# Both expert stages of a two-layer diffusion block in groups of four experts of one token stream

## The chip, the cores and the metric

The kernel runs on one core of one Trainium2 chip. The metric is the device time of one execution in microseconds; the profile's span, from the first to the last instruction, lies inside it.

## The reference, cut to the expert stage

A layer is a mixer (attention or a recurrence) followed by a mixture of experts. Layer 0 runs the experts on two token streams of 256 tokens each (context and latent), layer 1 on the latent stream alone. Each token goes to 2 of 32 experts; an expert is a gate, an up and a down matrix of 1024 x 256, 1024 x 256 and 256 x 1024 in fp32.

```python
def hier_moe(h, w_rg, b_rg, w_re, b_re, w_gate, w_up, w_down):
    ...
    y = jnp.zeros_like(x)
    for g in range(MOE_GROUPS):
        a = jax.nn.silu(jnp.einsum('td,edf->tef', x, w_gate[g])) * jnp.einsum('td,edf->tef', x, w_up[g])
        y = y + jnp.einsum('tef,efd->td', a * comb[:, g, :, None], w_down[g])
    return y.reshape(b_, n, d)

def reference(...):
    for layer in range(DEPTH):
        ...
        x = x + g1 * o_lat
        x = x + g2 * hier_moe(ada_modulate(x, norm2_g[layer], sh2, sc2), *moe_p)
        if not last:
            xc = xc + g1c * o_ctx
            xc = xc + g2c * hier_moe(ada_modulate(xc, norm2_g[layer], sh2c, sc2c), *moe_p)
    return rmsnorm(x, final_norm_g)
```

## The kernel before

The expert stage (`moe`) does not run every token through every expert. Each expert has 32 slots (`CAP`) per stream. `gather` multiplies one-hot matrices with the normed tokens and so collects the tokens of eight (layer 0) or four (layer 1) experts as columns of a tile `X`. `experts` works on a *pack*, 128 columns of `X`: in layer 0 two experts with 64 columns each, 32 of either stream; in layer 1 four experts with 32 columns.

- **Gate and up** (L1670, tile `gu`): `X` is the stationary operand, 128 x 64 in layer 0 and 128 x 32 in layer 1; the expert's weight streams past it, 256 columns. Matmuls of two experts alternate (`for j in es`, two entries), so two column blocks of the array work side by side. A matmul in fp32 is two instructions in the trace.
- **Turn** (`aT`, L1680): the product of gate and up is transposed.
- **Down** (L1697, tile `y`): stationary 128 x 32, 512 columns stream past. In layer 0 four blocks are side by side (two streams of two experts), in layer 1 two.
- **Scatter** (L1748, tile `sc`): `y` times the gate vector is split into a high and a low fp32r part, which in layer 0 stand on the upper and lower 64 partitions of one tile `z`, so that one matmul with a selection matrix brings both back to the tokens; VectorE adds the result to `x` (L1751). In layer 1, fp32 without a split.

Weights come by `fetch` (L1483), one DMA of 1 MiB each, issued by SyncE (SP) in the order of `start_loads`: `g g u u` of two experts at a time, the `d` of a pack after the `g` and `u` of the next one. They land in a rotation of *slots* of 1 MiB (`wm`): load number i takes the slot of load i minus the number of slots, and SP waits until the matmuls that read that slot are done. In layer 0 there are 14 slots (rings of 4 and 4, and `YRING` 6), in layer 1 21. All but one are filled ahead of a test (`tc.If(cnt > cap)`, L1453) on whether any expert has more than 32 tokens of a stream. In these inputs none has, and the body of the test, which repeats the work for the surplus, is skipped; every engine passes the test. What follows the end of the body needs every semaphore at the count that the body would have left.

The instructions are put in order on each engine by a scheduler with a simulated timeline of its own; it may move a load past the test.

Of the kernel before, what the change touches and what calls it, by code (L numbers as in the profile page):

```python
# [15 lines left out]
P = 128  # L16
# [76 lines left out]
class K:  # L93
# [3 lines left out]
    YRING = (6, 2)  # L97
    YG = 1
# [7 lines left out]
    OH = (1, 2)  # L106
    ET = (1, 1)
    ZP = 0
    XP = 1
    WP = (0, 2)  # L110
    YS = 1
# [11 lines left out]
    AB = 1  # L123
# [223 lines left out]
    def gate2(self, layer):  # L347
        self.g2 = self.cst.tile([P, D], F32, name="g2", tag="ms25")
        h = P // (2 - layer)
        for n, c in enumerate((0,) if layer else (1, 0)):  # L350
            self.nc.sync.dma_start(self.g2[n * h:n * h + h], cv2(self.md[layer], c * 4 * D + 3 * D, [[0, h], [1, D]]))
# [137 lines left out]
    def outproj(self, layer, wout, tiles):  # L489
# [81 lines left out]
        side = self.gather(self.rv, [0, 1], self.X, part=[0]) if layer == 0 else iter(())  # L571
# [669 lines left out]
    GRP = (256, 128)  # L1241
# [4 lines left out]
    def moe_open(self, layer):  # L1246
# [6 lines left out]
        self.cw = self.S * self.CAP  # L1253
        self.ne = P // self.cw
        self.grp = self.GRP[layer]
# [140 lines left out]
    def moe(self, layer):  # L1396
        nc = self.nc
        V = nc.vector
        cap, nt, ne = self.CAP, self.nt, self.ne
# [10 lines left out]
        cmx = self.counts()  # L1410

        n, m = 32 * self.cw // self.grp, self.grp // P

        def whole(rv):
            self.rank_rows(rv)
            w = 2 - layer
            groups = [list(range(t, t + w)) for t in range(0, n, w)]
            X = self.X
            old, prev = iter(()), iter(())
            for g, nxt in zip(groups, groups[1:] + [[]]):  # L1420
                gen = self.gather(rv, nxt, X) if nxt else iter(())
                packs = [(t, pk) for t in g for pk in range(m)]
                for t, pk in packs:
                    cur = self.experts((t * m + pk) * ne, X[t], pk, ne, self.load)
                    next(cur)
                    drain(old)
                    next(prev, None)
                    next(cur)
                    if layer:
                        for _ in range(KD // m):  # L1430
                            next(gen, None)
                    elif (t, pk) == packs[-1]:
                        drain(gen)
                    old, prev = prev, cur
                drain(gen)
            next(old, None)
            next(prev, None)
            drain(old, prev)

        def more(rv, grp):  # L1440
            self.rank_rows(rv)
            for t in range(grp * m, grp * m + m):
                X = {}
                self.over = self.px.tile([P, 2, 1024], F32, name="over", tag="yl")
                drain(self.gather(rv, [t], X, over=True))
                drain(self.experts(t * ne, X[t], 0, ne, self.load_one))

        if not layer:
            drain(self.gather(self.rv, [0, 1], self.X, part=[1]))
        elif self.GF:  # L1450
            drain(self.gather(self.rv, [0], self.X))
        cnt = nc.values_load(cmx[0:1, n:n + 1], min_val=0, max_val=2 * P)
        with self.tc.If(cnt > cap):  # L1453
            rv2 = p.tile([P, nt, 32], F32, name="rv2")
            V.tensor_copy(rv2, self.rv)
            for grp in range(n):
                es = slice(grp * 32 // n, (grp + 1) * 32 // n)
                cg = nc.values_load(cmx[0:1, grp:grp + 1], min_val=0, max_val=2 * P)
                with self.tc.For_i(cap, cg, cap):
                    V.tensor_scalar_add(rv2[:, :, es], rv2[:, :, es], -float(cap))  # L1460
                    more(rv2, grp)
        self.prefetch(1)
        if layer and not self.GF:
            drain(self.gather(self.rv, [0], self.X))
        whole(self.rv)
# [93 lines left out]
    def ranks(self, s):  # L1559
# [12 lines left out]
        g = 32 * self.cw // self.grp  # L1572
        V.tensor_reduce(self.cm[:, s, :g], pc[:, :32].rearrange("p (g e) -> p g e", g=g), axis=AX.X, op=ALU.max)

    def counts(self):
        V, p = self.nc.vector, self.mp
        g = 32 * self.cw // self.grp
# [17 lines left out]
    def gather(self, rv, ts, out, over=False, part=None):  # L1595
        nc, p = self.nc, self.p
        cap, nt, S, cw, ne = self.CAP, self.nt, self.S, self.cw, self.ne
        part = list(range(S) if part is None else part)
        grp = P if over else self.grp
        n1, m = grp // cw, grp // P  # L1600
        n, e0 = n1 * len(ts), n1 * ts[0]
        if ts[0] not in out:
            for t in ts:
                q, tag = (self.px, "xt0") if S == 1 else (self.mp, f"xt{t % 2}")
                out[t] = (self.over[:, 0].rearrange("p (k c) -> p k c", k=KD) if over else q.tile([P, KD, grp], F32, name="X", tag=tag, bufs=1),
                          self.mp.tile([P, m], F32, name="ws", tag="wso" if over else "ws", bufs=4), {})
        X, ws, oh = out[ts[0]]
        for s in part:
            both = self.mp.tile([P, 2, n, cap], F32R if S > 1 else F32, name="onehot", tag="oh0", bufs=nt // 2)
            for i in range(0, 2, self.OH[self.layer]):  # L1610
                j = slice(i, i + self.OH[self.layer])
                nj = self.OH[self.layer]
                nc.vector.tensor_tensor(both[:, j], self.iob[:, :cap].unsqueeze(1).unsqueeze(1).to_broadcast([P, nj, n, cap]),  # L1613
                                        rv[:, 2 * s + i:2 * s + i + nj, e0:e0 + n].unsqueeze(3).to_broadcast([P, nj, n, cap]), op=ALU.is_equal)
            oh[2 * s], oh[2 * s + 1] = both[:, 0], both[:, 1]
        for k in range(KD):
            o = self.ps("xg")[:, :len(part) * n * cap]
            for q, s in enumerate(part):
                os = o[:, q * n * cap:(q + 1) * n * cap]
                for i in (2 * s, 2 * s + 1):  # L1620
                    r = oh[i].rearrange("p e s -> p (e s)")
                    hs = [self.h2h[:, i, k]] + ([self.h2l[s][:, i % 2, k]] if S > 1 else [])
                    for n_, h in enumerate(hs):
                        nc.tensor.matmul(os, h, r, start=i % 2 == 0 and n_ == 0, stop=i % 2 == 1 and n_ == len(hs) - 1)  # L1624
            q0 = k - (KD - m * len(ts))
# [155 lines left out]
```

## Time and profile before

| | before |
|---|---|
| device time, three runs | 1153.53, 1154.44, 1156.45 us |
| span of the profiled execution | 1152.0 us |
| TensorE (PE) busy | 1033.0 us, 90% |
| VectorE (DVE), ScalarE (ACT), GpSimd busy | 603.2, 426.1, 250.2 us |
| read from HBM | 292.98 MB, 255 GB/s over the span |
| layer 0's expert matmuls | from 390.5 us to about 660 us |
| layer 1's expert matmuls | from 904.2 us to the end |

The profiled execution has no device time of its own beside its span; the median of the three runs is 2.4 us above the span. Times in the trace are microseconds from the start of the span. Matmul ends in the trace are modelled, so how fast a group of matmuls runs is read from starts: the start of the group to the start of what follows.

### The profile page before, as it was taken

The numbers are of one execution on the slowest core, as the hardware profiler recorded it, in microseconds if no ns is written. First come the engines' busy times: TensorE is split into PE (matmuls) and PEld (weight loads), VectorE is DVE, ScalarE is ACT, GpSimd is POOL, SyncE is SP. The second block draws the span as 40 slices with busy tenths as digits, with TensorE's granted clock in tenths as the row PEclk, the third lists the DMA queues.
The fourth block names the chain that finished last, engine by engine and source line by source line (L and its number), as shares of the span: only waits on it lengthen the run. The fifth ranks groups of instructions, "written<-read, shape, count | busy, mean of one in ns | idle before, by whom it ended". The sixth has DMA issues, their size and how long they took to land. (4 is left out here: it accounts for less than half of the span.)

```text
span 1152.0 us, 19666 instructions
## 1 busy us (share of the span) xinstructions
PE 1033.0 (90%) x7917; PEld 644.9 (56%) x7917; DVE 603.2 (52%) x1261; ACT 426.1 (37%) x769; POOL 250.2 (22%) x283
## 2 busy tenths in 40 slices
PE   4998796979896699999999787999997799999996
PEld 3766573757674456565564365566654565444442
DVE  4349776577467347686667851344676122212223
ACT  4354455547545323242232352446555110000002
POOL 2216463426306000000000165343420000000000
PEclk9999798989998799999999989999999899999999
DMA  9883435344445299999979756642477599999920
GB/s 307 278 303 134 161 125 198 110 154 145 148 176 232 98 418 376 423 406 371 420 319 343 226 172 181 216 168 110 136 232 318 219 420 419 420 422 419 420 83 37
DMA packets 99183, 295.57 MB, mean 257 GB/s; under 512 B 23000, under 2 KB 57040, under 8 KB 74368
## 3 DMA queue, kind: packets, MB, share of 16 engines
q1 hardware_dynamic: 97360, 292.64, 67.7%
q10 hardware_dynamic: 1200, 1.26, 0.4%
q8 instruction: 67, 1.10, 0.4%
q0 software_dynamic: 512, 0.21, 0.1%
q14 instruction: 44, 0.36, 0.1%
HBM read 292.98 MB, written 1.11 MB: 255 GB/s over the span
## 5 line engine op out<-in xcount | busy, mean ns | idle before, releaser
L1670 PE MATMUL gu<-g,X 128*64 128x256 f32 (+1 forms) x1024 | 126.9, 392 | 9.0 <-DVE rq L1588 4.7
L1697 PE MATMUL y<-d,aT 128*32 128x512 f32 x768 | 131.6, 596 | 0.2
L1751 DVE TENSOR_TENSOR x<-sc,x 128x512 f32<-128x512 f32 x156 | 99.5, 685 | 50.1 <-PE sc L1748 49.9
L1670 PE MATMUL gu<-u,X 128*64 128x256 f32 (+1 forms) x1024 | 120.6, 380 | 0.0
L1735 POOL COPY esel<-idb 32x64 bf16<-32x64 bf16 (+1 forms) x40 | 11.2, 300 | 439.3 <-PE bc L1736 397.5
L1670 PEld LDWEIGHTS gu<-g,X 128*64 128x64 f32 (+1 forms) x1024 | 67.3, 126 | 54.0 <-issue 12.4
L1670 PEld LDWEIGHTS gu<-u,X 128*64 128x64 f32 (+1 forms) x1024 | 68.4, 123 | 44.3 <-issue 3.2
L1675 ACT ACTIVATE sge<-gu 128x256 f32<-128x256 f32 x24 | 9.2, 384 | 190.6 <-PE gu L1670 190.6
L1624 PE MATMUL xg<-onehot,h2h 128*128 128x128 f32 (+1 forms) x384 | 68.5, 294 | 3.6 <-DVE onehot L1613 1.7
L1697 PEld LDWEIGHTS y<-d,aT 128*32 128x32 f32 x768 | 31.9, 109 | 70.4 <-issue 62.9
L1748 PE MATMUL sc<-z,sc 128*128 128x512 f32 x184 | 65.2, 482 | 4.0 <-DVE z L1727 4.0
L183 PE MATMUL pt<-hh,wl 128*128 128x512 f32 (+1 forms) x160 | 61.2, 383 | 7.6 <-POOL wl L177 6.4
L181 PE MATMUL pt<-hh,wh 128*128 128x512 f32 (+1 forms) x160 | 63.7, 398 | 1.2 <-ACT hh L430 0.6
L1634 ACT ACTIVATE X<-xg,ab 128x128 f32<-128x128 f32 x104 | 42.0, 458 | 61.4 <-PE xg L1624 43.6
L1624 PEld LDWEIGHTS xg<-onehot,h2h 128*128 128x128 f32 x384 | 57.0, 200 | 13.3 <-issue 8.8
L1676 DVE SCALAR_TENSOR_TENSOR sge<-gu,ws,sge 128x256 f32<-128x256 f32 x24 | 11.5, 479 | 96.5 <-ACT sge L1675 96.5
L182 PE MATMUL pt<-hl,wh 128*128 128x512 f32 (+1 forms) x160 | 60.7, 379 | 0.8 <-DVE hl L432 0.8
L1725 ACT CAST z<-yg 64x512 fp32r<-64x512 f32 x64 | 39.5, 617 | 48.9 <-DVE yg L1719 44.2
L1636 DVE TENSOR_SCALAR X<-xg,ab 128x128 f32<-128x128 f32 x88 | 33.0, 407 | 46.9 <-PE xg L1624 46.1
L177 POOL TENSOR_TENSOR wl<-wcol,wh 128x512 fp32r<-128x512 f32 (+1 forms) x32 | 41.1, 1288 | 55.7 <-ACT wh L174 54.9
L1727 DVE TENSOR_TENSOR z<-yg,z 64x512 fp32r<-64x512 f32 x64 | 43.9, 686 | 17.3 <-ACT z L1725 16.0
L1748 PEld LDWEIGHTS sc<-z,sc 128*128 128x128 f32 x184 | 31.9, 189 | 33.5 <-issue 17.7
(402 smaller groups left out, 2056.3 us busy)
## 6 DMA issues: line engine op xcount, KB each, us to landing
g<-in_moe_w_gate_dram SPq DMA_DIRECT2D x64, 1024.0 KB, 10.8
u<-in_moe_w_up_dram SPq DMA_DIRECT2D x64, 1024.0 KB, 11.9
d<-in_moe_w_down_dram SPq DMA_DIRECT2D x64, 1024.0 KB, 11.3
wada<-in_ada_w_dram SPq DMA_DIRECT2D x48, 1024.0 KB, 6.2
wcol<-in_ab_w_in_dram SPq DMA_DIRECT2D x8, 1024.0 KB, 8.8
wcol<-in_cd_w_in_dram SPq DMA_DIRECT2D x5, 1024.0 KB, 12.0
wtok<-in_ab_w_in_dram SPq DMA_DIRECT2D x4, 1024.0 KB, 5.5
wout<-in_ab_w_out_dram SPq DMA_DIRECT2D x4, 1024.0 KB, 8.7
```

The costliest lines, as they stand in the source:

```text
L177: (el or nc.vector).tensor_tensor(lo, src, hi.bitcast(F32), op=ALU.subtract)
L181: mm(out, lh, rh, start=start, stop=False, **kw)
L182: mm(out, lh, rl, start=False, stop=False, **kw)
L183: mm(out, ll, rh, start=False, stop=stop, **kw)
L1624: nc.tensor.matmul(os, h, r, start=i % 2 == 0 and n_ == 0, stop=i % 2 == 1 and n_ == len(hs) - 1)
L1634: nc.scalar.activation(xv[:, s], o[:, j, q], AF.Identity, scale=a2, bias=b2)
L1670: A.matmul(pg[r, c0:c0 + 256], X[:, k, (pk * ne + j) * cw:(pk * ne + j + 1) * cw], ws[j][:, k % (KD // parts), :], start=k == 0 and c0 == ...
L1697: A.matmul(py[hf][r:r + cap, :], aT[:, k, q:q + cap], ws[j][:, k - k0, hf * 512:(hf + 1) * 512], start=k == 0, stop=k == 1)
L1725: S.copy(Z[s][a, cs], yg[a])
L1727: eng.tensor_tensor(Z[s][b, cs], yg[a], Z[s][a, cs].bitcast(F32), op=ALU.subtract)
L1748: A.matmul(o, sc[:, n * P:(n + 1) * P], z[:, cs], start=z is zs[0] and not last, stop=z is zs[-1])
L1751: V.tensor_tensor(self.xi(i)[:, cs], o, self.xi(i)[:, cs], op=ALU.add)
```

## The change

Both layers work on *quads*, four experts of one stream: 128 columns are 4 experts x 32 slots of one stream. A quad in layer 0 has both streams one after the other, each with its own `X`, `gu`, `aT`, `y` and `z`. Gate, up and down all have 128 x 32 stationary operands and four blocks side by side. The high and low parts of `z` are two tiles of 128 partitions, whose two matmuls add up in the accumulator. The first quad's gate and up in layer 0 stand ahead of the test, stream by stream. `YRING` goes from 6 to 4 in layer 0, which leaves 12 slots. Loads come as `g` x4, `u` x4, then the `d` x4 of the quad before. The second stream's gate vector is a tile of its own (`g2b`), loaded from GpSimd's queue.

```diff
-    YRING = (6, 2)
+    YRING = (4, 2)
+    NQ4 = 8
+    ZB = 4
...
     def start_loads(self, layer, head):
-        ne = P // ((2 - layer) * self.CAP)
         self.order = []
-        for e0 in range(0, 32, ne):
-            for h in range(e0, e0 + ne, 2):
-                self.order += [(k, h + j) for k in "gu" for j in range(2)]
-            if e0:
-                self.order += [("d", e0 - ne + j) for j in range(ne)]
+        for q in range(self.NQ4):
+            self.order += [(k, 4 * q + j) for k in "gu" for j in range(4)]
+            if q:
+                self.order += [("d", 4 * q - 4 + j) for j in range(4)]
...
+        if layer:
+            drain(self.gather(self.rv, 0, 4, 0, self.X))
+            cur = None
+        else:
+            drain(self.gather(self.rv, 0, 8, 1, self.X))
+            cur = self.quad(0, self.X, segs, self.load)
+            self.gate_up(cur, by_seg=True)
+        cnt = nc.values_load(cmx[0:1, nq:nq + 1], min_val=0, max_val=2 * P)
         with self.tc.If(cnt > cap):
...
+        for q in range(nq):
+            end = q == nq - 1
+            if cur is None:
+                cur = self.quad(q, self.X, segs[::-1] if end else segs, self.load)
+                self.gate_up(cur)
+            Q[q], cur = cur, None
+            if S > 1 and q % 2 and not end:
+                for s in segs:
+                    drain(self.gather(self.rv, 4 * q + 4, 8, s, self.X))
+            if q > 1:
+                self.scatter(Q[q - 2], segs)
+            if q:
+                self.down(Q[q - 1], segs)
+            self.turned(Q[q])
+            if S == 1 and not end:
+                drain(self.gather(self.rv, 4 * q + 4, 4, 0, self.X))
+        self.scatter(Q[nq - 2], segs[::-1])
+        for s in segs[::-1]:
+            self.down(Q[nq - 1], [s])
+            self.scatter(Q[nq - 1], [s])
...
+        def mms(key, c0, s, k0, ws):
+            X, _, q0 = st["X"][s]
+            x0 = (q - q0) * P
+            for k in range(k0, k0 + kn):
+                for j, w in ws.items():
+                    A.matmul(pg[s][32 * j:32 * j + 32, c0:c0 + 256], X[:, k, x0 + 32 * j:x0 + 32 * j + 32], w[:, k - k0, :],
+                             start=k == 0 and c0 == 0, stop=k == KD - 1, skip_group_check=True)
...
+        if by_seg:
+            ws = {key: {j: load(key, 4 * q + j) for j in range(4)} for key in "gu"}
+            for s in segs:
+                for key, c0 in (("g", 0), ("u", 256)):
+                    mms(key, c0, s, 0, ws[key])
+                mid(s)
+            return
+        for h in range(0, 4, step):
+            for key, c0 in (("g", 0), ("u", 256)):
+                for k0 in range(0, KD, kn):
+                    ws = {j: load(key, 4 * q + j, k0, k0 + kn) for j in range(h, h + step)}
+                    for s in segs:
+                        mms(key, c0, s, k0, ws)
...
+                z = (zz[:, hf * D:hf * D + D] if last else p.tile([P, D], F32R, name="z", tag="z", bufs=self.ZB)).rearrange("p (a c) -> p a c", a=2)
+                yg = self.yg[:, cs] if last else p.tile([P, 512], F32, name="yg", tag="yg", bufs=2)
+                V.tensor_tensor(yg, py[s, hf], self.g2[s][:, cs], op=ALU.mult)
+                self.split(yg, z[:, 0], z[:, 1])
+                st["z"][s, hf] = [z[:, 0], z[:, 1]]
...
+                    for m, z in enumerate(zs):
+                        nc.tensor.matmul(o, st["sc"][:, n * P:(n + 1) * P], z, start=m == 0 and not last, stop=m == len(zs) - 1)
+                    if not last:
+                        nc.vector.tensor_tensor(self.xi(i)[:, cs], o, self.xi(i)[:, cs], op=ALU.add)
```

**SP at the test of layer 0.** The load queue of the kernel before: the last two loads issued ahead of the test, the test, the end of its body, and the first loads behind it (`g_5`, `u_4`: gate of expert 5, up of expert 4; the brackets name the queues and engines that a row waits for).

```order
L1483 DMA g_5_3555<-in_moe_w_gate_dram 128x2048 [waits DMAHW5_49]
L1483 DMA u_4_3557<-in_moe_w_up_dram 128x2048 [waits DMAHW6_49]
L1452 TENSOR_LOAD cmx [waits DVE_49]
L1453 COMPARE_AND_BRANCH
...
L1453 UNCONDITIONAL_BRANCH [waits SP_sequencer_49,DMAHW0_49,DMAHW1_49,DMAHW2_49,DMAHW3_49,DMAHW4_49,DMAHW5_49,DMAHW6_49,DMAHW7_49]
L1483 DMA u_5_7520<-in_moe_w_up_dram 128x2048 [waits DMAHW2_49,DMAHW6_49,DVE_49,DMAHW7_49,PE_49,Activation_49]
L1483 DMA d_2_7715<-in_moe_w_down_dram 128x2048 [waits DMAHW0_49,PE_49]
```

The same place of the changed kernel.

```order
L1479 DMA g_6_3562<-in_moe_w_gate_dram 128x2048 [waits DMAHW3_49]
L1429 TENSOR_LOAD cmx [waits DVE_49]
L1479 DMA u_4_7531<-in_moe_w_up_dram 128x2048 [waits DMAHW4_49,PE_49]
L1479 DMA u_5_7533<-in_moe_w_up_dram 128x2048 [waits DMAHW5_49,PE_49]
L1479 DMA u_6_7535<-in_moe_w_up_dram 128x2048 [waits PE_49]
L1479 DMA u_7_7537<-in_moe_w_up_dram 128x2048 [waits DMAHW7_49,PE_49]
L1479 DMA d_0_7757<-in_moe_w_down_dram 128x2048 [waits DMAHW0_49,PE_49]
L1479 DMA d_2_7761<-in_moe_w_down_dram 128x2048 [waits DMAHW2_49,PE_49]
L1430 COMPARE_AND_BRANCH
...
L1430 UNCONDITIONAL_BRANCH [waits SP_sequencer_49,DMAHW0_49,DMAHW1_49,DMAHW2_49,DMAHW3_49,DMAHW4_49,DMAHW5_49,DMAHW6_49,DMAHW7_49]
L1479 DMA g_7_7444<-in_moe_w_gate_dram 128x2048 [waits DMAHW2_49,DVE_49,DMAHW3_49,PE_49,Activation_49]
```

Seven loads (`u_4` to `u_7`, `d_0` to `d_2`) now stand between the reading of the count and the test, and `g_7`, which the second quad's gate needs first, stands behind the end of the body, where SP waits for all eight hardware queues.

**PE behind the test of layer 0**, changed kernel: the first quad's transposes, three of the second quad's four gates twice, then rows that do not need `g_7` (left out are 20 matmuls of the next gather), then `g_7`.

```order
L1683 MATMUL aT<-ident,sge 128x128
L1651 MATMUL gu<-g_4_3558,X 32x256 [waits DVE_49,DMAHW1_49,PE_49,Activation_49]
L1651 MATMUL gu<-g_5_3560,X 32x256 [waits DMAHW2_49]
L1651 MATMUL gu<-g_6_3562,X 32x256 [waits DMAHW3_49]
L1651 MATMUL gu<-g_4_3558,X 32x256 [waits PE_49]
L1651 MATMUL gu<-g_5_3560,X 32x256
L1651 MATMUL gu<-g_6_3562,X 32x256
L1584 LDWEIGHTS rq [waits DVE_49]
...
L1651 MATMUL gu<-g_7_7444,X 32x256 [waits DMAHW3_49]
L1651 MATMUL gu<-g_4_3558,X 32x256
```

In the kernel before, the first pack's gate (`g_0`, `g_1`) stands at this place; in the changed one the whole first quad's gate and up stand ahead of the test.

**PE in layer 1**, gate matmuls of experts 20 to 23 in the kernel before and of 16 to 19 in the changed one.

```order
L1670 MATMUL gu<-g_21_14611,X 32x256
L1670 MATMUL gu<-g_20_14609,X 32x256
L1670 MATMUL gu<-g_21_14611,X 32x256
L1670 MATMUL gu<-g_20_14609,X 32x256
L1670 MATMUL gu<-g_21_14611,X 32x256
```

```order
L1651 MATMUL gu<-g_18_14440,X 32x256
L1651 MATMUL gu<-g_19_14442,X 32x256
L1651 MATMUL gu<-g_16_14436,X 32x256
L1651 MATMUL gu<-g_17_14438,X 32x256
L1651 MATMUL gu<-g_18_14440,X 32x256
```

Two experts alternated; now four do, on the four 32-column blocks of the array.

## Rows read from the trace of the kernel before

**Rows 1.** Page, parts 1 and 2: PE, and DMA busy tenths in 40 slices

```profile
PE 1033.0 (90%) x7917; PEld 644.9 (56%) x7917; DVE 603.2 (52%) x1261; ACT 426.1 (37%) x769; POOL 250.2 (22%) x283
DMA  9883435344445299999979756642477599999920
```

**Rows 2.** Windows: busy us by engine, PEclk, DMA share, GB/s

```profile
480.00:500.00 20.00, 20.00 (x159) 11.04 (x156) 13.40 (x22) 4.84 (x9) 0.51 (x3) 1.00 1.01 420
1038.00:1070.00 32.00, 31.85 (x221) 15.10 (x220) 7.07 (x14) 2.58 (x6) 0.28 (x1) 1.00 1.01 420
1070.00:1102.00 32.00, 31.86 (x221) 15.07 (x219) 7.06 (x14) 2.58 (x6) 0.28 (x1) 1.00 0.95 394
1102.00:1134.00 32.00, 31.88 (x194) 13.73 (x194) 8.94 (x15) 2.70 (x5) 0.00 (x0) 1.00 0.00 1
```

**Rows 3.** Chain that ended last, layer 1: start us, us, what

```profile
1014.41 9.01 PE gu L1670 x90
...
1110.30 9.01 PE gu L1670 x90
...
1130.42 3.43 PE xo L1686 x8
1133.86 5.35 PE y L1697 x32
...
1139.23 0.70 DVE yg L1719
```

**Rows 4.** Timeline of PE in layer 1: start us, us, line, operation, count

```profile
1017.64 2.98 PE L1670 MATMUL gu<-g,X 128*32 128x256 f32 x26
1020.44 2.98 PE L1670 MATMUL gu<-u,X 128*32 128x256 f32 x26
...
1025.44 1.95 PE L1624 MATMUL xg<-onehot,h2h 128*128 128x128 f32 x16
1027.32 3.62 PE L1697 MATMUL y<-d,aT 128*32 128x512 f32 x12
...
1038.89 3.70 PE L1748 MATMUL sc<-z,sc 128*128 128x512 f32 x8
1042.52 0.84 PE L1670 MATMUL gu<-g,X 128*32 128x256 f32 x6
```

**Rows 5.** Timeline of PE in layer 0, one pack, and a gather's two ends

```profile
414.10 3.67 PE L1670 MATMUL gu<-g,X 128*64 128x256 f32 x32
...
421.16 2.18 PE L1748 MATMUL sc<-z,sc 128*128 128x512 f32 x8
423.43 3.64 PE L1697 MATMUL y<-d,aT 128*32 128x512 f32 x32
427.00 0.51 PE L1680 MATMUL aT<-ident,sge 128*128 128x128 f32 x2
427.44 3.67 PE L1670 MATMUL gu<-g,X 128*64 128x256 f32 x32
...
440.91 0.37 PE L1624 MATMUL xg<-onehot,h2h 128*128 128x256 f32 x1
...
450.52 2.38 PE L1670 MATMUL gu<-g,X 128*64 128x256 f32 x20
```

**Rows 6.** Timeline of PE: four 32-column blocks side by side, 256 columns each

```profile
654.53 1.07 PE L333 MATMUL ada<-wada,c 128*32 128x256 f32 x16
```

**Rows 7.** Timeline of PE at layer 0's test, and windows there (clock)

```profile
385.43 0.72 PE L1648 MATMUL wslot<-wEs,onehot 128*32 128x1 f32 x40
390.47 5.79 PE L1670 MATMUL gu<-g,X 128*64 128x256 f32 x26 [4.32 <-DVEq L1453]
388.90:395.60 6.70, 5.13 (x24) 3.20 (x25) 1.57 (x5) 0.00 (x0) 0.40 (x2) 0.50 0.45 161
```

**Rows 8.** Loads: SP's timeline before the test; tile u, issue to landing

```profile
358.18 32.52 SPq L1483 DMA_DIRECT2D u<-in_moe_w_up_dram  x2
DMA to landing us min/median/max: 4.7/11.9/19.8
```

**Rows 9.** Timeline of PE at the end of layer 0's stage

```profile
642.57 0.50 PE L1680 MATMUL aT<-ident,sge 128*128 128x128 f32 x2
...
657.66 2.20 PE L1748 MATMUL sc<-z,sc 128*128 128x512 f32 x6 [2.06 <-DVE z L1727]
```

**Rows 10.** Page, part 5: scatter's additions on VectorE

```profile
L1751 DVE TENSOR_TENSOR x<-sc,x 128x512 f32<-128x512 f32 x156 | 99.5, 685 | 50.1 <-PE sc L1748 49.9
```

More of the change, by code (lines that the diff above doesn't have):

```diff
@@ L122 @@
     NE = (0, 0, 0)
-    AB = 1
     NYR = 4
@@ L570, in outproj @@
             evac(os_, 1, part)
-        side = self.gather(self.rv, [0, 1], self.X, part=[0]) if layer == 0 else iter(())
+        side = self.gather(self.rv, 0, 8, 0, self.X) if layer == 0 else iter(())
         self.moe_pair(segs[-1], p, st[segs[-1]], side)
@@ L1410, in moe, with more @@
         cmx = self.counts()
-        n, m = 32 * self.cw // self.grp, self.grp // P
-        def whole(rv):
+        segs = list(range(S))
+        if S > 1:
+            self.gate2(0, 1, p, nc.gpsimd)
+        def more(rv, q):
             self.rank_rows(rv)
[L1416 to L1438, printed above, removed]
@@ L1452, in moe @@
-        cnt = nc.values_load(cmx[0:1, n:n + 1], min_val=0, max_val=2 * P)
+                drain(self.gather(rv, 4 * q, 4, s, X, over=True))
+                st = self.quad(q, X, [s], self.load_one)
+                self.gate_up(st)
+                self.turned(st)
+                self.down(st, [s])
+                self.scatter(st, [s])
+        if layer:
[5 more added lines that the diff above has]
+            self.gate_up(cur, by_seg=True)
@@ L1593, in rank_rows @@
         nc.scalar.copy(self.rqT[0:32], o[0:32, :nt * P])
[L1595 to L1615, printed above, removed]
-        for k in range(KD):
[L1617 to L1625, printed above, removed]
-            if q0 >= 0 and S - 1 in part:
-                self.slot_weights(out, ts, oh, q0, e0, m)
-            o = o.rearrange("p (s t e r) -> p t s e r", s=len(part), t=len(ts), e=n1)
-            for j, t in enumerate(ts):
-                xv = out[t][0][:, k].rearrange("p (e s r) -> p s e r", s=S, e=n1)
-                for q, s in enumerate(part):
-                    b2, a2 = self.ab[:, s, 0, k:k + 1], self.ab[:, s, 1, k:k + 1]
-                    if (j + k + s) % 2 or part == [0] and S > 1:
-                        nc.scalar.activation(xv[:, s], o[:, j, q], AF.Identity, scale=a2, bias=b2)
-                    else:
-                        nc.vector.tensor_scalar(xv[:, s], o[:, j, q], a2, b2, op0=ALU.mult, op1=ALU.add)
@@ L1652, in experts, with quad @@
-    def experts(self, e0, X, pk, ne, load):
+        for i in range(2):
+            for j in range(4):
+                e = 4 * c + j
+                nc.tensor.matmul(pw[32 * j:32 * j + 32, 0:1], both[:, i, e].bitcast(F32), self.wE[:, 2 * s + i, e0 + e:e0 + e + 1],
+                                 start=i == 0, stop=i == 1)
+        nc.vector.tensor_copy(ws[:, c:c + 1], pw[:, 0:1])
+    def quad(self, q, X, segs, load):
+        return dict(q=q, X={s: X[s] for s in segs}, segs=segs, load=load, parts=2 if load == self.load_one else 1,
+                    last=q == self.NQ4 - 1 and self.layer == 1 and load == self.load, z={})
@@ L1682, in experts @@
-        yield
+        q, parts, load, last = st["q"], st["parts"], st["load"], st["last"]
         if last:
@@ L1738, in experts @@
[L1738 to L1751 removed]
+            zz = self.wm("z", F32R)
```

249 lines of the change are left out of this document (120 added, 129 removed).

## The prediction

> **What bounds the kernel now.** I read the page's busy shares first: TensorE (PE) is busy for 90% of the span, no other engine for more than 52%, and the slices show the DMA engines full in two stretches, the two expert stages [rows 1]. So the question in each stage is whether PE or the transfers set the pace, and the windows answer it. In layer 0 (480 to 500) PE fills the whole stretch and the DMA engines are full beside it; in layer 1 (1038 to 1102) PE is again busy throughout, but the DMA share falls to 0.95 in the window that ends at 1102 and to nothing behind it [rows 2]. Transfers that are full and still done 50 us before the end mean that PE is the bound, but not by much: the chain that ended last is PE alone, its gate and up for experts 4q to 4q+3 recurring three periods apart at 1014.41 and 1110.30, so 31.96 us for four experts [rows 3], while their 12 loads of 1 MiB take 12 x 1.0486 / 0.42 = 30.0 us at the windows' 420 GB/s, 2.5 us each. That is the first number to keep: in layer 1 PE can lose at most 2 us per four experts before the transfers take over.
>
> **Layer 1, the change by parts.** Two-wide, 26 gate or up instructions take 2.80 us from start to start, 0.108 us each, so 128 take 13.8 us [rows 4]. No gate or up in the old kernel is four wide. The nearest row that is, with the same 256 columns in fp32, took 1.07 us for 16 [rows 6], 0.067 with its modelled tail (about 0.18 us) and 0.056 without it; half of the two-wide price is 0.054. I take 0.056: 7.2 us per quad, with 0.067 (8.6 us) as the dear end. Down takes 32 instructions in 3.57 us where it already is four wide, in layer 0 [rows 5]. A quad in layer 1 then needs 7.2 + 3.6 of down, two times 1.88 for its gather, 3.63 for its scatter [rows 4] and some 1.5 for the rest, about 20 us instead of 32. The transfers still need 30, so the kernel is rid of only a part: PE will wait for loads, and the stage ends where the transfers end plus what must follow them.
>
> When do they end? The 0.95 of 1.01 in the window from 1070 puts it at 1070 + 32 x 0.95/1.01 = 1100.1 [rows 2], and since the engines are full already, faster matmuls don't move that. The last four loads are the last quad's down; the four ahead of them land at 1090.1. PE then has down of quad 6 (3.6), the turn (0.5), scatter (3.6) and the output's transposes `xo` (3.4): 11.2 us, a little more than the 10 of the last loads. At layer 0's test PE came back from 4.3 us of idling at a granted clock of 0.50, that is 1.2 instead of 2.4 GHz, for 395.6 - 390.5 = 5.1 us, which lost 2.6 us [rows 7]; I add that, and 1 us for VectorE's split: 1090.1 + 11.2 + 3.6 = 1104.9. The last down (3.6) ends at 1108.5. In the old kernel it ended at about 1139.2, and 12.8 us followed to the end of the span [rows 3]; with the same tail the new end is 1121.3, so **layer 1 gives 31 us**. Bounds: 28 if waits in the last 10 us add up, 36 if the first quad frees its slots some 4 us sooner, so that the full stretch begins earlier.
>
> **Layer 0.** Gate and up cost the same there: 256 instructions at 0.054 are 13.8 us for a quad of two streams, against 2 x 7.06 for two packs [rows 5]. The scatter keeps 16 matmuls for 8 experts' worth of half-packs, down and the turns stay. VectorE is spared 64 additions of 685 ns [rows 10], 44 us, and the splits are halved, but it is busy for 13.4 of 20 us while PE doesn't wait [rows 2], so this is hidden behind PE and counts for nothing; if VectorE were the bound it would be the gain. What changes is the test. In the old kernel PE idled 4.3 us there [rows 7]. Now 256 instructions of gate and up stand ahead of it, from 386.0 to 399.9, and seven loads (`u_4` to `d_2`) stand on SP between the count and the branch. The first four wait for the slots of `g_0` to `g_3`, whose last use is at three quarters of this, about 396.5. A load on idle engines lands 4.7 us after its issue [rows 8], each further one 2.5 us later: 396.5 + 4.7 + 6 x 2.5 = 416.2. SP waits at the end of the skipped body for all eight hardware queues, so `g_7` leaves only then: 416.2 + 0.9 + 4.7 = 421.8. Behind the test PE has some 5 us of work that doesn't need `g_7` (turns, six gates, 20 of a gather's matmuls), and idles otherwise. So **PE takes up gate and up of quad 1 at about 421.8**; queued behind that one load are all of PE's later work and through it every other engine.
>
> From there: the old stage took from 390.47 to 657.66 + 2.20 = 659.86 [rows 7, 9], 269.4 us. Its parts account for 16 packs x 13.34 (414.10 to 427.44) and 3 gathers x 9.61 (440.91 to 450.52) [rows 5], together 242.2; of the other 27.2 us, 2.6 are the low clock, 2.1 the last wait [rows 9], and 22.5 are the gate vectors' spread (`bc`), the next layer's `ada` and the switches between kinds of matmul. The new stage lacks the first quad's gate and up (2 x 7.06 = 14.1), a turn (0.9) and a third of one gather (3.0). Blocks are twice as long and the selections 8 instead of 16, so a part of the 22.5 goes too: nothing at one end, half (11) at the other, and I take a third, 7. So 269.4 - 14.1 - 0.9 - 3.0 - 7 = 244.4 and the stage ends at 421.8 + 244.4 = 666.2: **layer 0 gives back 6 us**. With no switch saved it gives back 13. With half of them saved and the seven loads landing 4 us sooner it gains 2.
>
> Can the 12 slots hold it? A quad's 12 loads need 30.0 us, PE 244.4 / 7 = 34.9 on average. The four gates of the next quad can start when this quad's gate is done and land 4.7 + 3 x 2.5 = 12.2 us later; until they are needed PE has up, scatter, down and turn, about 20 us. The four ups come 10 us behind, 22.2 after that release, and are needed 7 us after the gates, at 27. So there is no wait, with 5 to 8 us to spare.
>
> The second gate vector, 512 KB on GpSimd's queue, is needed only by the first scatter and lies beside 40 us of gate and up. The mixers' matmuls stand as they stood.
>
> **Sum**, against the profiled execution: 1152.0 - 31 + 6 = 1127 of span. The median of the runs is 2.4 us above that span, so 1129.5; I say 1130.
>
> **The rivals.** *The pause at layer 0's test is mostly hidden*, because the loads start sooner than I have it or the longer blocks save more. The end is then 8 to 15 us earlier, 1115 to 1122. For it: the switches' 22.5 us are the least known term. Against it: `g_7` stands behind everything by order.
>
> *Layer 1 at the low clock.* A PE that waits for loads three times in a quad may come back at 0.50 each time, as it did at layer 0's test after 4.3 us [rows 7]. All of a quad's 20 us at half speed would be 40, more than the 30 of the transfers; but then PE would not wait, and what it did without waits ran at 1.00 [rows 2]. So it settles between: with 60% of the work at the low clock a quad takes 32 us, as now, and the whole gain is gone, 1152 + 6 + 2.4 = 1160. More likely some waits are caught up and 5 to 12 us are lost, 1135 to 1142. The Trainium skill ("TensorE: Matmul & The Clock Gate", section on HAM oscillation) describes this: bursts of matmuls that are shorter than the waits for data between them start at the low clock each time. By that rule alone the price in layer 1 would be in this rival's range; the one restart in rows 7 agrees with it, and no stretch of the old kernel shows such bursts.
>
> *Four wide isn't twice two wide.* At 0.067 instead of 0.054, the dear end of rows 6, layer 0's 1792 instructions behind the test cost 23 us more (1153); layer 1 hides it. Against it: down already runs 512 columns four wide at 0.112, half of which is 0.056 [rows 5]. The Trainium skill (same page, "Measured speedup vs the span model") has 2.38 times for three blocks of 32, which as an estimate for four would be near that dear end; the down row speaks against it here.
>
> *Slower than before: twelve slots hold PE in layer 0.* If each group of four loads pays the 4.7 us anew, since its slots come free together after the queue has run dry, a quad's loads take 30 + 3 x 4.7 = 44.1 us against PE's 34.9: 9.2 us for each of seven quads, 64 us, and 1194. It decides from 38.5 us of transfers per quad on (25 us over seven quads eat the net gain). For it: two slots fewer, and loads in fours instead of twos. Against it: the three releases fall in different parts of the quad, with the margins above.
>
> **How the numbers follow.** The forecast as summed, 1123 to 1135, has 0.50; the hidden pause 0.18; the low clock in layer 1, with gain left, 0.15; the price of four wide 0.06, partial in most cases, so 1137 to 1150; the slots 0.08, of which the most is above 1158; all gain gone by the clock 0.03. The range from 1112 to 1143 leaves out the last two, most of the fourth and the far ends: 0.8 inside. About 3.5 us, 0.3%, is what a measurement of this kernel can tell from no change. Faster by more than that has 0.88, the same 0.04, slower 0.08.
>
> **What would show it.** In layer 1: a period of 30 us, PE idle before gate, up and down on DMA, the DMA share at 1.01 to the end of the loads near 1107 on the new span, and a granted clock below 1.00 in places. In layer 0: PE idle for 15 to 20 us around the test, released by the DMA of a gate (`g_7`), then no DMA waits; two quads in about 70 us, and gate instructions four of which start every 0.22 us. VectorE's additions are 64 fewer at no gain. Wrong if PE waits for loads in layer 0 past 430, if layer 1's quads take over 31 us, or if PE restarts far from 422.

## The result, and the profile after

The changed kernel took 1121.88 us (median of four runs, 1117.34 to 1126.99) against 1155.39 for the kernel before in runs beside it, a ratio of 0.9713 (95% interval 0.9681 to 0.9745): 33.5 us faster. The forecast was 1130, with a range from 1112 to 1143. The profiled execution has a span of 1115.2 us; it is the quickest of the four runs, so the sums below, which are made against its span, come out some 3 us larger than those of the medians.

The page of the changed kernel, parts 1 and 2, the lines that answer to [rows 1] and the granted clock in 40 slices:

```profile
PE 976.0 (88%) x8933; PEld 617.7 (55%) x8933; DVE 533.1 (48%) x1133; ACT 394.9 (35%) x696; POOL 244.4 (22%) x260
PEclk9999798989999788999999998999999999989998
DMA  9984526236253265999989987764267759999994
```

The DMA engines are now full to the last slice but one, where [rows 1] has them at 2 tenths and at nothing in the last two. That is layer 1, and the windows say it in numbers (columns as in [rows 2]):

```profile
960.00:990.00 30.00, 26.15 (x247) 12.69 (x239) 7.07 (x14) 2.59 (x6) 0.28 (x1) 0.94 1.01 420
990.00:1020.00 30.00, 26.37 (x227) 12.35 (x223) 7.16 (x14) 2.58 (x6) 0.28 (x1) 0.90 1.01 420
1050.00:1080.00 30.00, 25.65 (x227) 12.24 (x223) 6.81 (x13) 2.58 (x6) 0.00 (x0) 0.96 1.02 421
1095.00:1100.00 5.00, 5.00 (x22) 1.88 (x24) 1.45 (x3) 0.00 (x0) 0.00 (x0) 1.00 0.40 159
```

PE has 26 us of work in 30 where it had 30, at a granted clock a little below 1, and the DMA share stays at 1.01 until 1095. The chain that ended last is no longer PE's [rows 3] but a row of loads (start, us, what):

```profile
915.41 6.94 PE gu L1651 x128
...
967.46 19.80 DMA u<-in_moe_w_up_dram
...
987.31 6.27 PE gu L1651 x57
...
997.26 19.82 DMA u<-in_moe_w_up_dram
...
1017.13 5.03 PE gu L1651 x57
```

From one of these quads to the next are 1017.13 - 987.31 = 29.82 us, where it took 31.96, and each of the two is released by its last `u`. From turn to turn the last four quads took 28.9 to 31.3 us, 30.1 on average. PE waits for `u` nine times in layer 1, 14.8 us in all, and but for 0.6 us on a `d` for no other load. In layer 0 the timeline of PE around the test (columns as in [rows 7]) shows the two stretches of idling, and the one of SP where `g_7` was issued:

```profile
397.43 3.64 PE L1651 MATMUL gu<-u,X 128*32 128x256 f32 x64
408.34 1.10 PE L1683 MATMUL aT<-ident,sge 128*128 128x128 f32 x4 [7.28 <-DVEq L1430]
409.37 1.93 PE L1651 MATMUL gu<-g,X 128*32 128x256 f32 x12
...
425.21 8.75 PE L1651 MATMUL gu<-g,X 128*32 128x256 f32 x113 [8.87 <-DMA g<-in_moe_w_gate_dram]
...
664.32 0.73 PE L1754 MATMUL sc<-z,sc 128*128 128x512 f32 x2 [0.62 <-DVE z L175]
```

```profile
397.62 2.00 SPq L1479 DMA_DIRECT2D u<-in_moe_w_up_dram  x4
401.07 1.30 SPq L1479 DMA_DIRECT2D d<-in_moe_w_down_dram  x3
420.36 0.34 SPq L1479 DMA_DIRECT2D g<-in_moe_w_gate_dram  x1
```

Where the 36.8 us of the two spans come from: the end of layer 0's last scatter moved from 659.86 to 664.32 + 0.73 = 665.05, 5.2 later. The mixer between the stages went from 244.3 us (659.86 to 904.2) to 236.1 (665.05 to 901.17), 8.2 less. Layer 1 from its first gate to the end of the span went from 247.8 to 214.0, 33.8 less.

### The profile page after: what moved, and what is told of

Same layout as the page of the kernel before. It is cut to its first block, busy times and chain, and to the rows that moved or that the text cites. A ratio compares the mean times of both kernels' runs of the same rounds, so it can differ in the third digit from the quotient of the medians.

```text
span 1115.2 us, 21435 instructions
## 1 busy us (share of the span) xinstructions
PE 976.0 (88%) x8933; PEld 617.7 (55%) x8933; DVE 533.1 (48%) x1133; ACT 394.9 (35%) x696; POOL 244.4 (22%) x260
## 5 line engine op out<-in xcount | busy, mean ns | idle before, releaser
L1651 PE MATMUL gu<-u,X 128*32 128x256 f32 x1536 | 104.6, 403 | 14.8 <-DMA u<-in_moe_w_up_dram 14.8
L1719 PE MATMUL y<-d,aT 128*32 128x512 f32 x768 | 115.8, 595 | 0.7 <-DMA d<-in_moe_w_down_dram 0.6
L1651 PE MATMUL gu<-g,X 128*32 128x256 f32 x1536 | 102.4, 394 | 13.5 <-DMA g<-in_moe_w_gate_dram 8.9
L1651 PEld LDWEIGHTS gu<-u,X 128*32 128x32 f32 x1536 | 57.8, 116 | 55.0 <-DMA u<-in_moe_w_up_dram 19.1
L1651 PEld LDWEIGHTS gu<-g,X 128*32 128x32 f32 x1536 | 53.7, 113 | 56.7 <-issue 17.9
L1617 DVE TENSOR_SCALAR X<-xg,ab 128x256 f32<-128x256 f32 (+1 forms) x64 | 29.8, 475 | 90.0 <-PE gu L1651 47.9
L1756 DVE TENSOR_TENSOR x<-sc,x 128x512 f32<-128x512 f32 x92 | 58.9, 684 | 22.7 <-PE sc L1754 22.6
L1615 ACT ACTIVATE X<-xg,ab 128x256 f32<-128x256 f32 (+1 forms) x64 | 32.0, 509 | 49.6 <-PE xg L1611 41.7
L172 ACT CAST z<-yg 128x512 fp32r<-128x512 f32 x34 | 20.9, 619 | 80.1 <-DVE yg L1736 71.6
L172 ACT CAST wh<-wcol 128x512 fp32r<-128x512 f32 (+1 forms) x42 | 25.6, 611 | 45.4 <-PE pt L180 35.1
```

The lines of the kernel that those rows point to most:

```text
L172: nc.scalar.copy(hi, src)
L1615: nc.scalar.activation(X[:, k], o, AF.Identity, scale=a2[:, k:k + 1], bias=b2[:, k:k + 1])
L1617: nc.vector.tensor_scalar(X[:, k], o, a2[:, k:k + 1], b2[:, k:k + 1], op0=ALU.mult, op1=ALU.add)
L1651: A.matmul(pg[s][32 * j:32 * j + 32, c0:c0 + 256], X[:, k, x0 + 32 * j:x0 + 32 * j + 32], w[:, k - k0, :], start=k == 0 and c0 == 0, stop= ...
L1719: A.matmul(py[s, hf][r, :], st["aT"][s][:, k, r], w[:, k - k0, hf * 512:(hf + 1) * 512], start=k == 0, stop=k == 1)
L1756: nc.vector.tensor_tensor(self.xi(i)[:, cs], o, self.xi(i)[:, cs], op=ALU.add)
```

## The experiments

Medians and ratios are against runs of the kernel before that ran beside them. "Mixer" is the time from the end of layer 0's last scatter to layer 1's first gate, "stage" from the first gate of layer 0 to the end of that scatter, both from the trace.

**The changed kernel again (`after_again`).**

> The changed kernel once more, for its spread and for a second trace. If the 8 us that the mixer between the two expert stages was shorter by (from the last scatter of layer 0 to the first gate of layer 1, 236 us after, 244 before) belong to the kernel's order, this trace has them again within 2 us; if they are chance, it has 240 to 244. Time 1117 to 1127.

1121.9 us (1118.47 to 1122.9), ratio 0.9707 (0.9689 to 0.9725). The mixer had 236.5 us again. Three more traces bear on it: `e2_two_wide_l1` and `e6_half_down` (below) have the changed kernel's order of work up to layer 1, `b2_layer1_four` has that of the kernel before, apart from the loads for layer 1. Their mixers took 236.5, 241.5 and 249.2 us. So either order has a short and a long mixer, some 5 us apart, and the orders differ by 8.

The 8 us are there early: from the end of layer 0's last scatter to the first matmul of the mixer's attention scores (tile `smla`) it is 73.6 to 74.1 us in the four traces of the new order, 81.6 and 81.8 in the two of the old. They belong to the order. The 5 us come late, mostly by the clock that TensorE was granted. Windows from 858 to 866 (columns as in [rows 2]), first `e6_half_down`, then the changed kernel:

```profile
858.00:866.00 8.00, 7.50 (x27) 3.83 (x28) 5.19 (x13) 4.42 (x10) 0.00 (x0) 0.61 0.68 260
858.00:866.00 8.00, 7.55 (x42) 4.50 (x41) 6.14 (x16) 5.43 (x13) 0.00 (x0) 1.00 0.82 327
```

PE is as busy in both, but gets 27 instructions done instead of 42. In `e6_half_down` the clock is at 0.50, that is 1.2 GHz, from 859.8 to 866.6, which as an estimate costs half of these 6.8 us, 3.4 of the 5. Why it fell in one execution and not in another of the same order isn't shown.

**The first quad behind the test (`e1_test_first`).** One edit of the changed kernel, for layer 0:

```diff
-            cur = self.quad(0, self.X, segs, self.load)
-            self.gate_up(cur, by_seg=True)
+            cur = None
```

> The changed kernel with the first quad's gate and up of layer 0 behind the test again, the rest as changed. Theory: the idling around the test is due to the seven loads that wait for those matmuls and are queued ahead of g_7. Without them g_7 is issued some 5 us after 387 and lands near 397, while PE comes back at 391, does 14 us of gate and up (2.6 more at the low clock) and goes on without a wait at about 408; with the 5 us of work that lay in the idling this stands against 425.2, so 12 us less: about 1110. Rival: the transfers hold layer 0 and the idling only moves into the stage; then 1119 to 1126, and PE waits for gate or up behind the test.

1117.4 us (1114.43 to 1121.54), ratio 0.9677 (0.9652 to 0.9702): 4.5 faster than `after_again`, not 12. The timeline of PE shows that the idling around `g_7` is gone, as the theory had it:

```profile
393.43 3.64 PE L1650 MATMUL gu<-g,X 128*32 128x256 f32 x32 [4.60 <-DVE rq L1580]
...
411.30 7.11 PE L1650 MATMUL gu<-g,X 128*32 128x256 f32 x128
418.23 7.09 PE L1650 MATMUL gu<-u,X 128*32 128x256 f32 x128
```

The second quad's gate starts at 411.3 instead of 425.2; with some 3.3 us of work that the other kernel has behind it there, 10.6 us are won. But the stage ends at 660.2, only 4.8 earlier. Nothing in between waits on DMA (the rival's sign); so some 6 us are lost in PE's own work, most of them in the down matmuls. Summed from start to start over the stage, the 512 down instructions took 68.9 us here, 64.0 in the changed kernel and 60.8 in the kernel before, against 57 when four run side by side all the time. The order of PE shows why, for experts 12 to 15:

```order
L1718 MATMUL y<-d_12_8689,aT 32x512 [waits DVE_49]
L1718 MATMUL y<-d_13_8691,aT 32x512
L1718 MATMUL y<-d_14_8693,aT 32x512 [waits DMAHW7_49]
L1718 MATMUL y<-d_14_8693,aT 32x512 x2
...
L1718 MATMUL y<-d_15_8695,aT 32x512 [waits DMAHW0_49]
L1718 MATMUL y<-d_12_8689,aT 32x512
```

The scheduler starts with the experts whose matrix it believes to be there, so `d_14` stands three times in a row and other rows go in pairs: fewer than four blocks of the array are in use.

**Down matmuls kept together (`e7_down_together`, `e8_tie_small`).** Both add to `e1_test_first`, in layer 0, small matmuls that read the fourth matrix and write the first column of `y`; the real ones overwrite it. `e7` uses one of 128 columns for each half of each stream's `y`:

```diff
+                if parts == 1 and not self.layer:
+                    for s in segs:
+                        for hf in range(2):
+                            A.matmul(py[s, hf][:, 0:1], st["aT"][s][:, 0, :], ws[3][:, 0, 0:1], start=True, stop=True, skip_group_check=True)
```

> As e1_test_first, and in layer 0 four matmuls of one column for each quad, which read the fourth down matrix and write the first column of y, so that no down matmul of a quad can start before all four matrices are there. Theory: e1 got back only 5 of the 10 us that its test gave it, because down matmuls of single experts were put alone (69 us for all, against 57 side by side); together they take about 60, and the stage ends 6 to 8 us earlier: about 1110. Rival: the matmuls wait for the fourth matrix as long as they gain; 1115 to 1120.

1118.9 us (1113.12 to 1121.68), ratio 0.9657 (0.9606 to 0.9708): no gain over `e1_test_first`, the rival's number. The trace says why it is not the rival's reason. The down instructions fell to 62.2 us, and PE waits for no load in the stage, but the 64 added ones took 8.2 from start to start. So the price of the remedy ate it, and a cheaper one had to decide. `e8` has three of 32 columns in the place of one of 128:

```diff
+                            for j in range(3):
+                                r = slice(32 * j, 32 * j + 32)
+                                A.matmul(py[s, hf][r, 0:1], st["aT"][s][:, 0, r], ws[3][:, 0, 0:1], start=True, stop=True, skip_group_check=True)
```

> As e7_down_together, but with matmuls of 32 columns for the first three experts instead of 128 columns, which cost some 3 us in all instead of 8.2. Theory: the down matmuls of layer 0 take 62 us together as in e7, instead of 69, and the stage ends 3 to 5 us earlier than with e1_test_first, at 655 to 657. Rival: no gain, since what the fourth matrix makes them wait comes back; the stage ends at 659 or later. The mixer behind it may differ by up to 7 us either way, since its order differs; the stage decides.

1103.1 us (1100.59 to 1108.2), ratio 0.9522 (0.9478 to 0.9566). The stage ends at 653.3, 6.9 earlier than with `e1_test_first`, and the 512 down instructions take 57.8 us, with 2.7 for the 192 added ones. PE's timeline has them in one piece for a quad of two streams:

```profile
528.00 0.40 PE L1718 MATMUL y<-d,aT 128*32 128x1 f32 x21
...
528.28 7.05 PE L1724 MATMUL y<-d,aT 128*32 128x512 f32 x63
535.25 0.74 PE L1682 MATMUL aT<-ident,sge 128*128 128x128 f32 x4
```

7.3 us for 64, where `e1_test_first` needed some 11 for the quad of the order above (525.51 to 529.96 and 530.63 to 537.6, with two gates in between). Of the kernels here that do the whole work this is the quickest, 52 us below the kernel before and some 19 below the changed one. Of the 19, about 12 (11.7 by the ends of the stage) are the test and the down matmuls. The rest is not located: the traced execution took 1108.2 us, not 1103, and its mixer of 238.7 us is no shorter than the changed kernel's, with a stretch at a granted clock of 0.50 (846 to 852) that the other trace lacks.

**Two-wide gate and up in layer 1 (`e2_two_wide_l1`).**

```diff
-                        mms(key, c0, s, k0, ws)
+                        for js in ((0, 1), (2, 3)) if self.layer and parts == 1 else (ws,):
+                            mms(key, c0, s, k0, {j: ws[j] for j in js})
```

> The changed kernel, but in layer 1 gate and up alternate between two experts only (0, 1, then 2, 3); loads, down and scatter as changed. Gate and up of a quad then take 13.8 us instead of 7, PE's work is about 27 us of the transfers' 30. Theory: the transfers set layer 1's pace, so the time stays within 5 us of the changed kernel (1120 to 1127) and PE's waits for loads shrink. Rival: PE's own speed made the gain; then 8 x 6.8 us are lost, 1170 or more, beyond the kernel before.

1128.0 us (1126.34 to 1130.7), ratio 0.9759 (0.9735 to 0.9783). By the instructions' price PE lost 6.8 us a quad, 54 in all, and the kernel lost 6 of them, 1 us more than the theory allows. So the transfers do set the changed kernel's pace; but the trace shows that they no longer do here, by little:

```profile
990.00:1020.00 30.00, 29.85 (x217) 13.59 (x216) 7.00 (x14) 2.13 (x5) 0.29 (x1) 1.00 1.01 420
1080.00:1110.00 30.00, 29.88 (x193) 12.90 (x194) 9.18 (x15) 2.71 (x5) 0.00 (x0) 1.00 0.63 259
```

PE is full at a clock of 1.00, the loads end near 1098.7 (0.63 of 1.01 in the last window) with PE at work without a wait until long after, and layer 1 takes 223.4 us instead of 214.0. The last five turns start at 984.14 to 1098.53, four quads in 114.4 us: with PE never waiting for a load, its work in a quad is 28.6 us and not 27. Less the 6.8, the changed kernel's is some 22 and not 20: my sum for a quad was short by 2 us.

**Half of down's bytes in layer 1 (`e6_half_down`).**

```diff
-        self.nc.sync.dma_start(t, self.I[nm][self.layer, g, j].rearrange("(p k) f -> p (k f)", k=k))
+        w = self.I[nm][self.layer, g, j].rearrange("(p k) f -> p (k f)", k=k)
+        c = 1024 if self.layer and key == "d" else 2048
+        self.nc.sync.dma_start(t[:, 0:c], w[:, 0:c])
```

> The changed kernel, but in layer 1 only the first half of each down matrix is loaded, and both halves of the product use it; PE's instructions stay. 2.5 MiB less of 12 MiB... that is 10 MiB per quad, 25 us of transfers instead of 29.8, with PE at about 25 us of work. Theory: the transfers set layer 1's pace; the period of a quad falls to 25 or 26 us and the stage by some 28 to 35 us: 1087 to 1094. Rival: PE's work (about 25 us, with the low clock behind each wait) set it by itself; then the gain is under 10 us.

1095.3 us (1091.66 to 1096.32), ratio 0.9459 (0.9415 to 0.9504): 26.6 faster than the changed kernel. (It is 2 MiB less that makes 12 into 10.) Layer 1 takes 187.9 us, 26.1 less, from bytes alone; up to 974 its chain is PE's own, behind that a row of loads. Two turns of the part that PE sets itself (start, us, what):

```profile
949.94 0.43 PE aT L1685 x2
...
971.51 0.43 PE aT L1685 x2
```

They are 21.6 us apart, which is PE's work in a quad. The gain is a little under the 28 to 35 forecast because PE, not the loads, holds the early quads: it is busy for 30 of 30 us from 960 to 990, then for 27.0 and 26.3, and the last turns are 24.6 to 26.8 us apart.

**Layer 1 alone (`b2_layer1_four`).** The kernel before, in which layer 1's packs already hold four experts:

```diff
-            for h in range(e0, e0 + ne, 2):
-                self.order += [(k, h + j) for k in "gu" for j in range(2)]
+            for h in range(e0, e0 + ne, 2 + 2 * layer):
+                self.order += [(k, h + j) for k in "gu" for j in range(2 + 2 * layer)]
...
-        step = 2 // parts
+        step = (2 + 2 * layer if parts == 1 else 2) // parts
```

and in the down loop `2 // parts` in the place of `step` for the halves of the contraction.

> The kernel before the change, with layer 1 alone changed: its packs already hold four experts, and now gate, up and down of all four alternate, with the loads in the order g x4, u x4, d x4. Layer 0 and the mixers keep their instructions. Theory: layer 1 gives 31 to 34 us by itself, its quads come every 29.8 us and PE waits for up's loads, so the time is 1155.5 - 33 = 1122; the rest of the change is then worth nothing on balance (the stage of layer 0 ends 5 us later, the mixer behind it is 8 us shorter). Rival: layer 1's gain needs something else of the change (the gather's evictions, the selections); then it stays above 1130.

1123.1 us (1121.92 to 1125.91), ratio 0.9694 (0.9649 to 0.9739), against 0.9713 and 0.9707 for the whole change. Layer 1 takes 215.3 us and waits 14.7 us for the loads of up, 8 times and 2.1 us at the longest, as the changed kernel does (14.8, 9, 2.0). Three edited places bring all that the change brings. Layer 0's rewriting is worth nothing on balance: its stage ends 5.2 us later in the changed kernel, and the mixer behind it is 8.2 shorter.

**VectorE's additions twice (`e4_adds_twice`).**

```diff
-                        nc.vector.tensor_tensor(self.xi(i)[:, cs], o, self.xi(i)[:, cs], op=ALU.add)
+                        for _ in range(1 if self.layer else 2):
+                            nc.vector.tensor_tensor(self.xi(i)[:, cs], o, self.xi(i)[:, cs], op=ALU.add)
```

> The changed kernel with every addition of the scatter in layer 0 done twice, so that the experts' part counts double: 64 additions of 685 ns more, 44 us on VectorE, as many as the kernel before had. Theory: VectorE's savings in layer 0 lie behind PE, so at most 3 us are lost. Rival: the time that layer 0 kept in spite of the longer pause came from VectorE; then 15 us or more are lost, 1137 and up.

1132.4 us (1130.74 to 1135.56), ratio 0.9799 (0.9774 to 0.9825): 10.5 lost, between the two. The stage takes 289.8 us instead of 278.0. PE waits for the additions themselves, where it did not before (columns: us in total, times, longest):

```profile
PE y L1719 <- DVE x L1757: 5.6, 8, 1.6
```

Doubled additions come in bursts of 16 for each quad, and a burst reaches PE through the accumulators that it holds. So of 44 us on VectorE a quarter shows. "Hidden behind PE" was too strong: VectorE is busy for 116.6 of 200 us from 460 to 660 here, but inside a burst it is busy all the time. It doesn't say that the old kernel, with its additions spread over packs of half the size, paid for them; [rows 2] show PE without waits there.

**What shortened the mixer (`b0_nab_vector`, `b1_nab_first3`).** Both traces, PE's waits in the first part of the mixer, us 660 to 745, first of the kernel before, then of the changed one:

```profile
PE pt L183 <- POOL wl L177: 6.4, 3, 4.7
```

```profile
PE pt L181 <- POOL wl L175: 1.6, 1, 1.6
```

In the old kernel GpSimd stood 10.1 us for three loads of the tile `nab` with `wl`, which PE needs, queued behind; in the new order two more `wl` stand ahead of the second of them. `b0` puts all additions to `nab` of the kernel before on VectorE, `b1` the first three:

```diff
-            GP.tensor_tensor(bt, bt, pen.unsqueeze(1).to_broadcast([P, 6, 64]), op=ALU.add)
+            (V if h < 3 else GP).tensor_tensor(bt, bt, pen.unsqueeze(1).to_broadcast([P, 6, 64]), op=ALU.add)
```

> The kernel before the change, with the additions to the tile nab in the second mixer on VectorE instead of GpSimd. Theory: the 8 us by which the mixer between the expert stages was shorter in the changed kernel are GpSimd's waits for nab's loads, with the split wl queued behind them and PE waiting for wl (6.4 us); the change only reshuffled that queue. Then the old kernel's mixer falls from 245 to about 239 and the time by 4 to 8 us, 1147 to 1151. Rival: they come from the expert stage's end itself (its slots and loads); then the mixer stays at 243 to 245 and the time at 1155.

1159.5 us (1156.88 to 1162.46), ratio 1.0026 (1.0006 to 1.0046), so rather slower than before; mixer 250.4.

> The kernel before the change, with only the first three additions to nab on VectorE (those that GpSimd waits for ahead of wl), the others on GpSimd as before. Theory: PE's 6.4 us of waiting for wl go and nothing takes their place late in the mixer, where all eight additions on VectorE had cost 7 to 8 us; the mixer falls from 245 to 239 to 243. Rival: as there, PE waits for the next weights of ada instead; the mixer stays at 243 to 245 and the time within 2 us of 1155.5.

1152.9 us (1150.62 to 1158.0), ratio 0.9972 (0.9944 to 0.9999); mixer 244.2. In both the wait for `wl` is gone and another of nearly its size stands in its place; in `b1`:

```profile
PE ada L333 <- DMA wada<-in_ada_w_dram: 4.5, 1, 4.5
```

The first matmul of `smla` comes 79.9 us (`b0`) and 79.1 us (`b1`) into the mixer instead of 81.6, so 1.7 and 2.5 of the 8 us are won there. Behind it both traces have a stretch at a granted clock of 0.50 that the old kernel's has not, from 831 to 841 in `b0` and near 865 in `b1`; the whole mixers, 250.4 and 244.2, are therefore no measure of `nab`. Windows from 855 to 870, `b1`, then the kernel before:

```profile
855.00:870.00 15.00, 13.20 (x55) 7.50 (x55) 11.07 (x25) 7.68 (x18) 1.01 (x1) 0.77 0.54 211
855.00:870.00 15.00, 13.20 (x70) 8.14 (x70) 11.74 (x27) 9.58 (x21) 2.02 (x2) 1.00 0.60 236
```

So the theory that `nab` alone made the difference falls: it accounts for 2.5 us at most, which is also what `b1` gains by its median. The mixer's start hangs on several loads at once, and taking away the first wait shows the next. Which of the reordered loads gives the changed kernel its 8 us stays open; that they are an effect of order, and come with it again, is what the traces under `after_again` show.

## Why the prediction was right, and where it was off

**Layer 1: right in mechanism and nearly in size (31 forecast, 33.8 measured).** The transfers set the pace (`e2_two_wide_l1` and `e6_half_down` show it from both sides), the period is 29.8 us (30.1 on average), and the DMA's end did not move: it came 1097.0 - 901.2 = 195.8 us after the stage's first gate (0.40 of 1.01 in the last window), and 1100.1 - 904.2 = 195.9 before. The 2.8 us more are the end. I had the last down start 4.8 us behind the last load; it started 1.9 behind it, since the low clock that I added did not come: PE was busy from 1083 on but for 0.7 us, at 1.00 from 1085.

Two terms in it were wrong and hidden by the bound. The quad's "about 20 us" is some 22 (`e2_two_wide_l1`, `e6_half_down`), because the down matmuls are not four wide there either. The timeline of PE in one quad:

```profile
997.26 1.90 PE L1719 MATMUL y<-d,aT 128*32 128x512 f32 x4
999.10 2.05 PE L1611 MATMUL xg<-onehot,h2h 128*128 128x128 f32 x16
```

Four instructions of one expert take 997.26 to 999.10, 0.46 us each, against the 0.112 of [rows 5]; this quad's down takes 6.6 us and not 3.6. I had read from the order that the gates alternate in fours, and took the same for down without looking. And the low clock in layer 1, which I held for a rival, was there:

```profile
957.00:986.00 29.00, 26.45 (x264) 12.94 (x256) 7.07 (x14) 2.59 (x6) 0.57 (x2) 1.00 1.01 420
987.00:993.00 6.00, 5.69 (x56) 2.71 (x58) 0.00 (x0) 0.00 (x0) 0.00 (x0) 0.50 1.01 416
994.00:1016.00 22.00, 19.50 (x159) 9.25 (x155) 7.16 (x14) 2.41 (x6) 0.28 (x1) 1.00 1.01 421
```

After two waits for `u` (1.4 and 1.9 us, a pair of matmuls between them) the next 6 us run at 0.50. That costs some 3 us in this quad (1.2 in the window from 1050 to 1080, at 0.96) and no time that shows: the last load still ends 195.8 us behind the first gate. The Trainium skill ("TensorE: Matmul & The Clock Gate", section on HAM oscillation) has bursts of matmuls that are shorter than the waits for data between them start at the low clock each time. Here PE works for some 26 us of each 30 and waits for some 3 to 4, and the one restart shown came back at 0.50 all the same.

**Layer 0: the sum right (6 lost forecast, 5.2 measured), its parts off by some microseconds each way.** PE took up the second quad at 425.2 instead of 421.8: the gather ended 1.1 later, and the seven loads and `g_7` took the rest. From there the stage took 239.8 us and not 244.4: of the 22.5 us for gate vectors, `ada` and switches I had saved a third, and it was more like half, although down took 3.2 us longer (64.0 against 60.8). A restart 3.4 us late and a stage 4.6 us short nearly cancel, so that the sum came out is partly luck. Four wide gate and up came out as half of two wide, 64 instructions in 390.52 - 387.06 = 3.46 us, 0.054 each. The rival of the slots did not happen: from 460 on PE is full. The rival that four wide isn't twice two wide did not happen either.

**The mixer: the step that failed.** "The mixers' matmuls stand as they stood" was true of PE's order in the parts that I compared, and was taken for "the mixer takes as long". It took 8 us less, because the order of the other queues behind layer 0 had changed; which of the reordered loads did it stays open (above). This is the larger part of the forecast's error (8.2 of the 11.8 us between the forecast's span of 1127 and 1115.2). By its number alone, 1121.9 us lies in the band of the rival with the hidden pause (1115 to 1122) and just below that of the forecast as summed (1123 to 1135). But the pause was not hidden: PE idled for 7.3 and 8.9 us around the test. What lowered the time most is a term that the prediction put at nothing and no rival held; that the number fits the rival's band is chance.

**A point that I had not seen.** The test in layer 0 costs what I worked out, but undoing it gave 4.5 and not 12. It also moved loads, and with them the scheduler's choice which down matmul is ready first. Only `e8_tie_small`, which takes that choice away, got both.

## What to carry to other kernels

Work out what the transfers of a stage need before its matmuls are made faster: here 30 of 32 us, so that a PE twice as quick in gate, up and down could give 2 us a quad and the tail behind the loads, and three edited places did all of it. Where blocks of the array work side by side, look at the order row by row for every kind of matmul: a scheduler that starts whichever expert is loaded first undoes the packing without a wait showing anywhere, and tiny matmuls that need the last operand restore it, if they are cheap. And where the issuing queue waits for its loads at a test, as SP does here, a load queued ahead of the test holds up every load behind it, so put work ahead of such a point only if no load ahead of it waits for that work.

## What the runs showed of the hardware

- Four column blocks side by side give the whole factor: 0.46 us for each instruction of a down matmul alone, 0.112 with four, 0.108 and 0.054 for gate and up two and four wide. The Trainium skill ("TensorE: Matmul & The Clock Gate", section "Measured speedup vs the span model") has 2.38 for three blocks; the rows here are nearer to the number of blocks itself.
- The small matmuls that only wait were not free: 64 instructions with 128 stationary columns took 8.2 us from start to start (0.13 each), 192 with 32 columns 2.7 us (0.014 each).
- The same order of work can meet a granted clock of 0.50 in one execution and of 1.00 in another: `e6_half_down` and the changed kernel differ so at 858 to 866 us, `b2_layer1_four` and the kernel before at 863 to 869, and their mixers are some 5 us apart, mostly for it. It is a part of the spread of 1117 to 1127 us; how much was not measured.
